# High and low weight halves laid element by element beside each other in the feature-major blocks of a hybrid decoder layer

## The chip, the cores and the metric

The kernel runs on one core of one Trainium2 chip. The time is device microseconds of that core, the median over several runs. A profile of one execution on the chip gives, for every instruction, its engine, start and duration; the engines are named PE (TensorE, matmuls), PEld (TensorE's weight loads), DVE (VectorE), ACT (ScalarE), POOL (GpSimd) and SP (the queue that issues the loads from memory).

## The reference

One decoder layer over 256 tokens of 2,048 features, in float32: a mixer that runs an mLSTM and an RWKV-7 branch in parallel and merges them with sigmoid gates, a cross-attention into 256 memory tokens, and a channel mixer (a convolution of width 3 over tokens, a gated GELU). Each part is normed before and after and added to the residual stream.

```python
def reference(x, mem, ...):
    h = rms_norm(x, mix_pre_norm[l])
    y = hybrid_mixer(h, w_in[l], ...)              # 2048 -> 10536 columns, two recurrences, w_branch_a/b, w_out
    x = x + rms_norm(y, mix_post_norm[l])
    h = rms_norm(x, xattn_pre_norm[l])
    m = rms_norm(mem, mem_norm[l])
    x = x + rms_norm(cross_attention(h, m, xattn_wq[l], xattn_wkv[l], xattn_wo[l]), xattn_post_norm[l])
    h = rms_norm(x, ffn_pre_norm[l])
    x = x + rms_norm(conv_glu_ffn(h, ffn_w_up[l], ffn_conv_w[l], ffn_conv_b[l], ffn_w_down[l]), ffn_post_norm[l])
    return x

def conv_glu_ffn(h, w_up, conv_w, conv_b, w_down):
    u = h @ w_up                                   # 2048 -> 16384
    uc = conv_b + sum(conv_w[j] * shift_right(u, CONV_WIDTH - 1 - j) for j in range(CONV_WIDTH))
    gate, up = split_cols(uc, (D_FF, D_FF))
    return (jax.nn.gelu(gate, approximate=True) * up) @ w_down
```

Almost all of the arithmetic is products of 256 tokens with large weight matrices, which are read once from memory.

## The kernel before

**Split products.** TensorE multiplies in a reduced float32 format (`float32r`). To keep accuracy, every operand is split into a high half (rounded to that format) and a low half (the rest), and a product is three matmuls: high weight with high activation, high weight with low activation, low weight with high activation. All three add up in PSUM.

**Blocks and chunks.** The weights come in chunks of 512 KB, 128 partitions x 1,024 float32. `run()` goes through a list of blocks, and each block through its chunks. A block is of one of two kinds. In a feature-major block (`fm`) the weights are the stationary operand: TensorE loads 128 x 128 weights and streams 256 tokens (`hh`, `hl`, `fh`, `fl`, ...) past them, so the output has features on partitions. A chunk holds two rows of contraction (`kj`) by 512 features, so 2 x 4 x 3 = 24 matmuls of 256 columns. In a token-major block (`tm`) the activations are stationary and the weights stream, 512 columns at a time. Most of the kernel is feature-major: the mixer's input projection in large part, gates, branch and output projections, and the FFN's up projection; the FFN's down projection is token-major and ends the program.

**The path of a chunk.** `Feed.dma` issues its load into a `raw` buffer (four of them). `Feed.hi` has ScalarE cast it to the high half, `wh`; `Feed.lo` has VectorE subtract the cast from `raw` into the low half, `wl`. `run()` calls `feed.lo(i + 3)` while it works on chunk `i`, so the halves are made two to three chunks ahead. `wh` and `wl` are separate pools of four buffers, each of 1,152 float32 per partition; a cast waits until the matmuls have read the `wh` four chunks back, a subtraction until they have read the `wl` four chunks back, and the subtraction also waits for its own cast. The order of all instructions is written out by the program (there is no scheduler): `Spread` deals the side work of evacuations and the recurrences out between matmuls by a fixed budget of costs.

**Where a half lies in its buffer.** `Feed.staged` (L374) puts the 1,024 values of a half not at the buffer's start but `o` elements behind it: 0 in token-major blocks with 512 or more columns, 16 elsewhere (64 bytes). The buffers and the activations that the matmuls stream all start at a multiple of 128 bytes. For 19 chunks of the program a table `KICK` (L342), indexed by the chunk's number, shifts it otherwise: kind 0 puts the first row at 24 elements and the second 24 further than usual, kind 1 puts only the second row 8 further, kind 2 puts both at 24. All entries lie below chunk 244, so before the long run of the FFN's up projection is under way.

Of the kernel before, what the change touches and what calls it, by code (L numbers as in the profile page):

```python
# [10 lines left out]
F32R = mybir.dt.float32r  # L11
# [4 lines left out]
P = 128  # L16
# [129 lines left out]
def _layer(ctx, tc, nc, d, dbg):  # L146
# [5 lines left out]
    wp = ctx.enter_context(tc.tile_pool(name="wp", bufs=4))  # L152
# [9 lines left out]
    def big(name, shape=None, dt=F32):  # L162
        return mp.tile(shape or [P, KD, S], dt, tag="big", bufs=2, name=name)
# [79 lines left out]
    class Stat:  # L243


        def __init__(self, name, tag="ysb1", sq="au", apart=False):
            self.name, self.tag, self.sq, self.apart = name, tag, sq, apart
            self.rc = cp.tile([P, 2], F32, name=name + "_c")
            self.n = 0
            self.done = False  # L250
# [94 lines left out]
    class Feed:  # L345
        def __init__(self, order):
            self.kind = [k for k, s in order]
            self.src = [s for k, s in order]
            self.raw, self.st, self.nd, self.ns, self.nl = {}, {}, 0, 0, 0

            self.sm = [big(f"w0{i}", [P, 4, 2, 512]) for i in range(2)]

# [21 lines left out]
        def staged(self, name, r, i):  # L374


            k, c = r.shape[1:]
            kick = KICK.get(i)
            e = -(-c // 64) * 64
            o = 0 if c >= 512 and self.kind[i] == "tm" else 16  # L380
            if kick is not None:
                o, e = ((24, e + 24), (o, e + 8), (24, e))[kick]
            w = wp.tile([P, 1024 + 128], F32R, tag=name, bufs=4, name=name)
            return w[:, o:o + k * e].rearrange("p (k c) -> p k c", k=k)[:, :, 0:c]

        def hi(self, upto):
# [1714 lines left out]
```

## Time and profile before

| | |
|---|---|
| time, median of 3 runs (lowest, highest) | 1866.33 us (1866.29, 1867.76) |
| span of the profiled execution, first to last instruction | 1863.2 us |
| granted TensorE clock in it | 0.999 |
| matmuls | 14,934, TensorE busy 1853.5 us |
| VectorE busy | 1295.5 us, of which the 639 subtractions into `wl` (L421) 774.8 us |
| ScalarE busy | 1017.0 us, of which the 639 casts into `wh` (L391) 663.6 us |
| loads from memory | 347.01 MB, 187 GB/s over the span |

The profiled execution is one run of its own; its span is from the first to the last instruction and leaves out what lies around them. In the rows of the profile, the names stand as output<-inputs with the moving operand before the stationary one, so `fm<-fh,wh` is a feature-major matmul that streams `fh` past weights `wh`. Matmuls overlap in the pipeline: a duration of 277 ns for one says how long it was in flight, and the pace is what starts are apart. Nearly all matmuls stand under the one line of the helper that issues them (L181), so they are told apart by their tiles.

### The profile page before, as it was taken

Reading aid. Unit: us, or ns where it says so; the run is one execution under the profiler, and the core shown is the slowest. Engines: PE = TensorE matmul, PEld = TensorE weight load, DVE = VectorE, ACT = ScalarE, POOL = GpSimd, SP = SyncE. Lnnn points to the kernel's source line nnn. Section 1 sums busy time; section 2 is a strip of 40 time slices with the busy share of each in tenths; the row PEclk is TensorE's granted clock in tenths of the full one; section 3 lists DMA queues with packets and bytes.
Section 4 is the critical chain, followed back from the end, with each engine's and each line's share of the span. In section 5 each row is a group of like instructions: output and inputs, shape, how many; then the busy total and the mean of one; then the engine's idle time right before and its main releaser. Section 6 shows DMA issues by size and latency. Waiting matters only on the chain.

```text
span 1863.2 us, 36212 instructions
## 1 busy us (share of the span) xinstructions
PE 1853.5 (99%) x14934; PEld 1767.5 (95%) x14934; DVE 1295.5 (70%) x1832; ACT 1017.0 (55%) x1492; POOL 32.4 (2%) x62
## 2 busy tenths in 40 slices
PE   9999999999999999999999999999999999999998
PEld 9999988999999999999999999999999988888887
DVE  7789777566675857787766667776666775556555
ACT  6876445655454646665554455444445554545544
POOL 0000020000000000000000000000000000000000
PEclk9999999999999999999999999999999999999999
DMA  7556544344555765555666666666666666666664
GB/s 261 186 166 203 180 149 160 136 160 158 172 195 196 277 197 180 165 180 172 202 192 194 196 195 196 185 194 199 195 194 195 197 192 215 194 193 192 194 192 145
DMA packets 98198, 351.47 MB, mean 189 GB/s; under 512 B 11056, under 2 KB 11568, under 8 KB 97648
## 3 DMA queue, kind: packets, MB, share of 16 engines
q1 hardware_dynamic: 97168, 348.01, 58.6%
q8 instruction: 117, 1.92, 0.4%
q10 hardware_dynamic: 864, 1.15, 0.2%
q14 instruction: 49, 0.40, 0.1%
HBM read 347.01 MB, written 2.10 MB: 187 GB/s over the span
## 4 chain that ended last, share of the span: by engine, by line
PE 98%; DVE 1%; DMA 0%; issue 0%; ACT 0%; ACTq 0%; DVEq 0%
PE fm L181 68%; PE tm L181 25%; PE gram L181 0%; DVE wl L421 0%; PE Y L181 0%; DMA w<-in_w_in_dram 0%; PE num L181 0%; PE lv L181 0%; DVE ql L66 0%; PE X L181 0%; PE U L181 0%; PE zg L181 0%; DVE z L66 0%; PE zwa L181 0%; PE xsc L181 0%
## 5 line engine op out<-in xcount | busy, mean ns | idle before, releaser
L421 DVE TENSOR_TENSOR wl<-raw,wh 128x1024 fp32r<-128x1024 f32 (+1 forms) x639 | 774.8, 1218 | 412.7 <-ACT wh L391 406.5
L391 ACT CAST wh<-raw 128x1024 fp32r<-128x1024 f32 (+1 forms) x639 | 663.6, 1043 | 476.0 <-PE fm L181 362.5
L181 PE MATMUL fm<-fh,wh 128*128 128x256 f32 x2048 | 564.2, 277 | 0.6 <-DVE fh L66 0.6
L181 PE MATMUL fm<-fh,wl 128*128 128x256 f32 x2048 | 563.2, 276 | 0.0
L181 PE MATMUL fm<-fl,wh 128*128 128x256 f32 x2048 | 563.2, 276 | 0.0
L181 PEld LDWEIGHTS fm<-fh,wh 128*128 128x128 f32 x2048 | 383.6, 188 | 0.8 <-DVE fh L66 0.8
L181 PEld LDWEIGHTS fm<-fl,wh 128*128 128x128 f32 x2048 | 383.5, 188 | 0.0
L181 PEld LDWEIGHTS fm<-fh,wl 128*128 128x128 f32 x2048 | 383.5, 188 | 0.0
L181 PE MATMUL tm<-wh,as 128*128 128x512 f32 x1024 | 315.1, 389 | 0.0
L181 PE MATMUL fm<-hh,wh 128*128 128x256 f32 x1024 | 284.3, 280 | 1.7 <-ACT wh L402 1.5
L181 PE MATMUL fm<-hl,wh 128*128 128x256 f32 x1024 | 281.7, 277 | 0.0
L181 PE MATMUL fm<-hh,wl 128*128 128x256 f32 x1024 | 281.5, 277 | 0.1
L181 PEld LDWEIGHTS tm<-wh,as 128*128 128x128 f32 x1024 | 192.2, 188 | 39.8
L181 PE MATMUL tm<-wl,as 128*128 128x512 f32 x512 | 199.2, 389 | 0.0
L181 PEld LDWEIGHTS fm<-hh,wh 128*128 128x128 f32 x1024 | 191.9, 188 | 3.4 <-ACT wh L402 1.7
L181 PEld LDWEIGHTS fm<-hl,wh 128*128 128x128 f32 x1024 | 191.9, 188 | 0.1
L181 PEld LDWEIGHTS fm<-hh,wl 128*128 128x128 f32 x1024 | 191.5, 188 | 0.3 <-DVE wl L421 0.3
L181 PEld LDWEIGHTS tm<-wl,as 128*128 128x128 f32 x512 | 96.1, 188 | 19.9
L66 ACT CAST as<-ac 128x256 fp32r<-128x256 f32 x128 | 45.6, 404 | 110.8 <-PE tm L181 110.8
L66 DVE TENSOR_TENSOR as<-ac,as 128x256 fp32r<-128x256 f32 x128 | 48.6, 421 | 61.7 <-ACT as L66 61.7
L181 PE MATMUL fm<-mgh,wh 128*128 128x256 f32 x256 | 70.9, 277 | 0.0
L181 PE MATMUL fm<-mgl,wh 128*128 128x256 f32 x256 | 70.8, 276 | 0.0
(406 smaller groups left out, 2225.0 us busy)
## 6 DMA issues: line engine op xcount, KB each, us to landing
raw<-in_w_fu_dram SPq DMA_DIRECT2D x256, 512.0 KB, 4.1
raw<-in_w_in_dram SPq DMA_DIRECT2D x152, 512.0 KB, 3.6
raw<-in_w_fd_dram SPq DMA_DIRECT2D x128, 512.0 KB, 3.9
raw<-in_w_br_dram SPq DMA_DIRECT2D x32, 512.0 KB, 4.1
raw<-in_w_mo_dram SPq DMA_DIRECT2D x32, 512.0 KB, 4.3
raw<-in_w_xk_dram SPq DMA_DIRECT2D x8, 512.0 KB, 4.2
raw<-in_w_xv_dram SPq DMA_DIRECT2D x8, 512.0 KB, 3.6
raw<-in_w_xq_dram SPq DMA_DIRECT2D x8, 512.0 KB, 4.0
```

The costliest lines, as they stand in the source:

```text
L66: return f(out, *a, **k)
L181: pe.matmul(out, lhsT, rhs, start=start, stop=stop, skip_group_check=True)
L391: nc.scalar.copy(wh, r)
L421: nc.vector.tensor_sub(wl, r, self.st[self.nl][0])
```

## The change

The two halves of a chunk get one buffer of 2,304 float32 instead of two of 1,152, from a pool of four (`w2`), allocated when the high half is made. In a feature-major chunk the high value and the low value of one weight are neighbours: high at even places, low at odd ones. Each half is then a view with a step of two elements, and so a weight load of 128 columns reads every second float32, 8 bytes apart, over 1,024 bytes. The cast writes, and the subtraction reads and writes, with the same step. The chunk starts 16 elements (64 bytes) into its buffer as before, or 24 if the table `KICK` has an entry for it, of whichever kind; the second row no longer has a shift of its own. In the other chunks the two halves lie one behind the other in the shared buffer and keep their offsets and kinds of shift. Sizes, the number of instructions and their order on every engine stay as they are.

```diff
@@ class Feed
             self.raw, self.st, self.nd, self.ns, self.nl = {}, {}, 0, 0, 0
+            self.pairs = {}
...
@@ def staged(self, name, r, i):
             k, c = r.shape[1:]
             kick = KICK.get(i)
             e = -(-c // 64) * 64
+            if name == "wh":
+                self.pairs[i] = wp.tile([P, 2304], F32R, tag="w2", bufs=4, name="w2")
+            w = self.pairs[i]
+            if self.kind[i] == "fm":
+                o = 16 if kick is None else 24
+                return w[:, o:o + 2 * k * e].rearrange("p (k c i) -> p k c i", k=k, i=2)[:, :, 0:c, name == "wl"]
             o = 0 if c >= 512 and self.kind[i] == "tm" else 16
             if kick is not None:
                 o, e = ((24, e + 24), (o, e + 8), (24, e))[kick]
-            w = wp.tile([P, 1024 + 128], F32R, tag=name, bufs=4, name=name)
+            w = w[:, 0:1152] if name == "wh" else w[:, 1152:2304]
             return w[:, o:o + k * e].rearrange("p (k c) -> p k c", k=k)[:, :, 0:c]
```

What waits for what shifts a little with the shared buffer. On VectorE, in the FFN's up projection, two subtractions with the work between them stood like this before (`raw` is the loaded chunk, `us` and `fm` belong to the evacuation of a finished block, and the names in brackets are what the instruction waits for):

```order
L421 TENSOR_TENSOR wl<-raw,wh 128x1024 [waits DMAHW4_49,PE_49,Activation_49]
L66 TENSOR_TENSOR us<-fm,stf_b 128x512 [waits PE_49]
L421 TENSOR_TENSOR wl<-raw,wh 128x1024 [waits DMAHW5_49,PE_49,Activation_49]
L66 TENSOR_TENSOR us<-fm,stf_b 128x512
L66 SCALAR_TENSOR_TENSOR tg<-us,cv,tg 128x255 [waits Activation_49]
```

and stand like this now:

```order
L428 TENSOR_TENSOR w_17711<-raw,w_17711 128x1024 [waits DMAHW4_49,Activation_49]
L66 TENSOR_TENSOR us<-fm,stf_b 128x512 [waits PE_49]
L428 TENSOR_TENSOR w_17749<-raw,w_17749 128x1024 [waits DMAHW5_49,Activation_49]
L66 TENSOR_TENSOR us<-fm,stf_b 128x512
L66 SCALAR_TENSOR_TENSOR tg<-us,cv,tg 128x255 [waits Activation_49]
```

The order is unchanged; the subtraction no longer waits for TensorE itself, since its buffer was already free when the cast before it wrote there. The cast in turn waits for one matmul more than before, the last that reads the low half of the chunk four back.

## The prediction

> **What bounds the kernel now.** I read the head of the page first, then its chain that ended last.
>
> ```profile
> span 1863.2 us, 36212 instructions
> PE 1853.5 (99%) x14934; PEld 1767.5 (95%) x14934; DVE 1295.5 (70%) x1832; ACT 1017.0 (55%) x1492; POOL 32.4 (2%) x62
> PEclk9999999999999999999999999999999999999999
> PE 98%; DVE 1%; DMA 0%; issue 0%; ACT 0%; ACTq 0%; DVEq 0%
> ```
>
> TensorE is busy 99% of the span at a full granted clock, and 98% of the chain is TensorE. Next is what TensorE itself waited for: the view of waits, TensorE's rows.
>
> ```profile
> PE fm L181 <- ACT wh L402: 1.5, 1, 1.5
> PE warm L181 <- POOL ones L210: 1.1, 1, 1.1
> PE fm L181 <- ACT wh L391: 0.2, 1, 0.2
> ```
>
> The three columns are microseconds in total, times, and the longest. After the first chunk, TensorE never waits for a weight half in any amount that counts. So only the pace of the matmuls can move the time. The chain in order of time gives that pace:
>
> ```profile
> 529.91 127.96 PE fm L181 x1128
> ...
> 938.94 568.50 PE fm L181 x5016
> 1507.44 348.20 PE tm L181 x1536
> ```
>
> One unbroken stretch of feature-major matmuls (names `fm`, 256 moving columns) takes 568.50/5016 = 113.3 ns each; the token-major one (`tm`, 512 columns) takes 348.20/1536 = 226.7 ns. The second is twice the first although each has one weight load of 128 columns. A pace proportional to the moving columns, 0.443 ns per column in both, is the pace of the moving stream; a pace set by weight loads would be the same in both. That is the main reading on which the forecast rests.
>
> How much room is left for the weight load, next? Weight loads by form (mean ns behind the busy time):
>
> ```profile
> L181 PEld LDWEIGHTS fm<-fh,wh 128*128 128x128 f32 x2048 | 383.6, 188 | 0.8 <-DVE fh L66 0.8
> L181 PEld LDWEIGHTS gbc<-g,id 4*128 4x128 f32 x8 | 1.0, 182 | 0.1
> L181 PEld LDWEIGHTS Y<-T,KR 64*64 64x64 f32 x96 | 3.0, 134 | 0.2
> L181 PEld LDWEIGHTS lv<-mt,m 32*32 32x32 f32 x128 | 2.3, 107 | 0.3
> ```
>
> From 32 to 64 columns a load grows by 27 ns, from 64 to 128 by 54 ns: 0.84 ns per column, and about 80 ns that overlap with the load before. 128 columns stream in 54/64 x 128 = 108 ns, against 113.3 ns of moving. The cover is thin: 5 ns, or 5% of a load's stream. A load that became 6% slower would set the pace.
>
> And the weight load can disturb the moving stream even when it is short enough. TensorE in order of time, the first and the last of 37 consecutive matmuls, and then of 16:
>
> ```profile
> 431.02 0.28 PE L181 MATMUL fm<-hh,wl 128*128 128x256 f32 x1
> ...
> 435.25 0.28 PE L181 MATMUL fm<-hh,wl 128*128 128x256 f32 x1
> ```
>
> ```profile
> 50.56 0.28 PE L181 MATMUL fm<-hh,wh 128*128 128x256 f32 x1
> ...
> 52.37 0.28 PE L181 MATMUL fm<-hh,wh 128*128 128x256 f32 x1
> ```
>
> 4.23 us over 36 gaps is 117.5 ns; 1.81 us over 15 gaps is 120.7 ns. The second stretch, and the later half of the first, are chunks 18 and 138, whose weights the table `KICK` (L342) puts 96 bytes behind a 128-byte boundary in place of 64. The code gives those matmuls no other difference, so the two reads of TensorE do interact, by where the weights lie against the moving operand. The earlier half of the first stretch (chunk 137, unshifted) is slow too: it follows 32 small matmuls. It looks as if TensorE could fall out of step after an interruption and stay so until a shifted chunk.
>
> **The change, part by part.** First its reach: every matmul that writes an `fm` tile.
>
> ```profile
> 0.00:1864.00 1864.00, 1301.41 (x11328) 1.00 0.59 189
> 938.90:1507.40 568.50, 568.50 (x5016) 1.00 0.63 194
> 0.00:938.90 938.90, 732.87 (x6313) 1.00 0.56 185
> ```
>
> These rows are busy time by stretch of the matmuls on `fm`: 11,328 in all. Each of their weight loads now reads 128 values over 1,024 bytes instead of 512. One nanosecond more per load, once the cover of 5 ns is gone, is 11.3 us.
>
> *The 8-byte step itself.* No matmul in this trace has weights with a step of two elements. The nearest row on one side is `gbc`, whose weights have step zero (one element, read 128 times): 182 ns against 188 for 128 neighbouring ones, so the load's time does not depend on how many bytes 128 columns cover, at least downwards. On the other side the nearest rows are the two out-of-step stretches: +4.2 ns (117.5 - 113.3) and +7.4 ns (120.7 - 113.3) per matmul, which on 11,328 matmuls is +48 and +84 us. I take the value of the first, no extra time, since a load that takes one value per step of 0.84 ns is what the 32-, 64- and 128-column rows and the step-zero row all show; both ends stay in the range.
> The Trainium skill, "SBUF — State Buffer", Specifications (TRN2), speaks against the change: SBUF lines are 16 bytes, at least two hits per line are needed for full bandwidth, and each new line costs. At 8 bytes a line still gets exactly two float32 hits, so by the letter the sum stays at zero, while the new lines per load double; no run here shows the line size.
> The same page, Who interferes with whom, calls the matmul and weight-load ports independent and says TensorE waits on nobody. The two stretches above disagree, with 117.5 and 120.7 ns against 113.3; by the rule alone the change would be worth exactly zero.
>
> *Pace of the two reads.* The moving operand steps 4 bytes per 0.443 ns, 9.0 bytes per ns. The weights stepped 4 bytes per 0.84 ns, half as fast; now they step 8, 9.5 bytes per ns, nearly equal. A fixed offset (64 bytes as before; 68 for the low half) then holds through the whole load. Either the two never meet, and the slow stretches go, or they meet all the time. What the first is worth: the table has 19 entries of 24 matmuls or less, 19 x 24 x 4.2 ns = 1.9 us, and some unshifted stretches beside them; an upper bound is everything that feature-major matmuls lose before 938.9 us, 732.87 - 6313 x 0.1133 = 17.6 us, most of it refills behind small matmuls that the change does not touch. I put it at 3 us, near the lower end, because a stretch of 1,128 matmuls there (127.96 us, 113.4 ns each) already runs at full pace.
>
> *The shifts.* In feature-major chunks three kinds of shift become one (24 elements, 96 bytes). Cost as now: 0.1 us each if they slow their own chunk.
>
> *Writes and waits.* The cast and the subtraction write every second element, and the subtraction reads so. Rows of the steady stretch, in order of time:
>
> ```profile
> 1195.65 1.23 DVE L421 TENSOR_TENSOR wl<-raw,wh 128x1024 fp32r<-128x1024 f32 x1 [1.50 <-ACT wh L391]
> 1197.28 1.05 ACT L391 CAST wh<-raw 128x1024 fp32r<-128x1024 f32 x1 [1.67 <-PE fm L181]
> 1000.00:1400.00 400.00, 400.00 (x3532) 400.00 (x3531) 274.62 (x365) 199.69 (x256) 0.00 (x0) 1.00 0.64 194
> ```
>
> A chunk is 24 x 113.3 ns = 2.72 us of TensorE, and 400 us hold 147 chunks. VectorE is busy 274.62 of the 400, ScalarE 199.69, so a subtraction could grow by (400 - 274.62)/147 = 0.85 us and a cast by 1.36 us before they set the pace. Below nothing there is no gain: neither is waited for. I take zero. If the subtraction doubled, VectorE would need 274.62 + 147 x 1.23 = 455 us for 400: 14% on 568 us, about +78 us.
> Waits: high and low half now share one buffer, so a cast waits for the last low-half matmul of the chunk four back, one matmul (0.11 us; 0.23 in token-major) later than now; the subtraction no longer waits for TensorE, being behind the cast already. Behind the cast on ScalarE stand the next casts; they are needed some two chunks (5 us) later, so 0.23 us is hidden. The order of instructions is the same on every engine.
>
> *Sum.* 11,328 x 0 - (0 to 3 us) + 0. The profiled span is 1863.2 us, 3.1 us under the 1866.33 median, which lies outside the first and last instruction; so 1862 of span, about 1865 us.
>
> **The rivals.**
> - *Out of step for long (slower).* Nothing ties the single 96-byte shift to the places where TensorE falls out of step with the new pace. For: chunk 137 shows that an unshifted chunk can be slow from start to end. Against: most unshifted chunks are not. Place: the long stretch from 938.94; price 5016 x 4.2 ns = 21 us, so 1887; it decides if the last interruption before that stretch leaves TensorE out of step.
> - *The weight load becomes the bound (slower).* From 6% more time per load, in all feature-major matmuls. For: the cover is 5 ns and the load covers twice the bytes; the moving stream, which already covers that many bytes, needs 113.3 ns for them. Against: the step-zero row. Price by the first stretch +48 us, 1914; by the second +84 us, 1950; one value per two of today's steps would be +0.84 x 128 = +108 ns, less 5 of cover, 1.2 ms, which I give next to nothing.
> - *The floor falls (faster).* If the 113.3 ns were itself the price of two reads colliding, matmuls could go down to the load's 108 ns: 11,328 x 5.3 = 60 us, 1806. Against: the 512-column matmuls pay the same per column with half as many loads.
> - *All losses before 938.9 us vanish (faster):* at most 17.6 us, 1849.
> - *VectorE's strided subtraction doubles (slower):* +78 us, 1944.
>
> **How the numbers follow.** About 0.2%, 3.7 us, is what a measurement of this kernel can tell from no change. Forecast, 1862.6 to 1870: 0.44. Out of step for long: 0.20. Load-bound: 0.18, of which 0.11 up to 1920. Floor falls: 0.10. All losses vanish: 0.05. VectorE: 0.03. So faster 0.10 + 0.05 = 0.15, within 0.2% 0.44, slower 0.20 + 0.18 + 0.03 = 0.41. The range 1850 to 1920 holds the forecast, the first rival, the cheaper part of the second and nearly all of the lost-time case: 0.44 + 0.20 + 0.11 + 0.05 = 0.80. The forecast's own range is 1862 to 1867.
>
> **What would show it.** Right: the long feature-major piece of the chain stays at 568 us for 5,016 matmuls, weight loads stay at 188 ns, and VectorE's subtraction at 1.23 us. Slow stretches gone: chunks 137 and 18 at 113 ns. Out of step: the same long piece at 117 ns or more in part. Load-bound: every `fm` matmul above 113.3 ns from the first chunk on, with longer weight loads and token-major matmuls unchanged at 226.7. Floor fallen: the piece under 560 us. What would make me wrong outright is a pace of the feature-major matmuls other than 113.3 ns in the long stretch.

## The result, and the profile after

The changed kernel takes 1936.14 us (median of 4 runs, 1935.76 to 1936.47); the kernel before took 1866.31 us beside it (median of 4). The ratio is 1.0375, 95% interval 1.036 to 1.039: 70 us slower, where about no change was forecast, and above the range of 1850 to 1920.

The head of the page and its chain, of the kernel after:

```profile
span 1934.0 us, 36171 instructions
PE 1925.6 (100%) x14934; PEld 1839.6 (95%) x14934; DVE 1297.5 (67%) x1832; ACT 1064.0 (55%) x1492; POOL 32.2 (2%) x62
PEclk9999999999999999999999999999999999999999
PE 99%; DMA 0%; ACT 0%; DVE 0%; ACTq 0%; issue 0%; DVEq 0%
```

TensorE is still the whole chain at the full granted clock, so the 70.8 us by which the span grew are matmuls that start further apart. The chain in order of time says which:

```profile
547.02 135.38 PE fm L181 x1128
...
976.09 601.92 PE fm L181 x5016
1578.01 348.44 PE tm L181 x1536
```

The long feature-major piece went from 568.50 to 601.92 us: 601.92/5016 = 120.0 ns a matmul in place of 113.3. The shorter one has the same pace, 135.38/1128 = 120.0. The token-major piece, whose loads the change leaves alone, stands at 348.44/1536 = 226.8 ns as before. The busy time of all matmuls on `fm`, and the forms of their weight loads:

```profile
0.00:1934.00 1934.00, 1373.75 (x11328) 1.00 0.58 182
```

```profile
L181 PEld LDWEIGHTS fm<-fh,w 128*128 128x128 f32 x4096 | 646.1, 194 | 0.8 <-DVE fh L66 0.8
L181 PEld LDWEIGHTS tm<-w,as 128*128 128x128 f32 x1536 | 288.1, 188 | 60.1 <-DVE w L428 0.3
```

The feature-major matmuls were busy 1301.41 us and are busy 1373.75: 72.3 us more, which is the whole loss. That is 6.4 ns for each of 11,328; the pace changed by 6.7 where it had been at its best. Their weight loads take 194 ns in place of 188, while those of the token-major matmuls stay at 188. The two other engines, by the groups of the page after, and last the cast of the page before:

```profile
L428 DVE TENSOR_TENSOR w<-raw,w 128x1024 fp32r<-128x1024 f32 (+1 forms) x639 | 775.7, 1218 | 492.2 <-ACT w L398 490.6
L398 ACT CAST w<-raw 128x1024 fp32r<-128x1024 f32 (+1 forms) x639 | 707.8, 1113 | 524.6 <-PE fm L181 394.4
L391 ACT CAST wh<-raw 128x1024 fp32r<-128x1024 f32 (+1 forms) x639 | 663.6, 1043 | 476.0 <-PE fm L181 362.5
```

The subtraction costs 1218 ns, as it did before, with a step in what it reads and writes. The cast grew from 1043 to 1113 ns, but ScalarE idles more than before, waiting for TensorE. Neither is what TensorE waits for.

### The profile page after: what moved, and what is told of

It is laid out like the page before. It is cut to its first block, busy times and chain, and to the rows that moved or that the text cites. A ratio compares the mean times of both kernels' runs of the same rounds, so it can differ in the third digit from the quotient of the medians.

```text
span 1934.0 us, 36171 instructions
## 1 busy us (share of the span) xinstructions
PE 1925.6 (100%) x14934; PEld 1839.6 (95%) x14934; DVE 1297.5 (67%) x1832; ACT 1064.0 (55%) x1492; POOL 32.2 (2%) x62
## 4 chain that ended last, share of the span: by engine, by line
PE 99%; DMA 0%; ACT 0%; DVE 0%; ACTq 0%; issue 0%; DVEq 0%
PE fm L181 70%; PE tm L181 24%; PE gram L181 0%; PE Y L181 0%; DMA w<-in_w_in_dram 0%; PE num L181 0%; PE lv L181 0%; PE X L181 0%; PE U L181 0%; PE zg L181 0%; PE xsc L181 0%; PE zwa L181 0%; PE xt L1927 0%; PE Tn L181 0%; PE stb L181 0%; PE xo L181 0%
## 5 line engine op out<-in xcount | busy, mean ns | idle before, releaser
L428 DVE TENSOR_TENSOR w<-raw,w 128x1024 fp32r<-128x1024 f32 (+1 forms) x639 | 775.7, 1218 | 492.2 <-ACT w L398 490.6
L398 ACT CAST w<-raw 128x1024 fp32r<-128x1024 f32 (+1 forms) x639 | 707.8, 1113 | 524.6 <-PE fm L181 394.4
L181 PE MATMUL fm<-fh,w 128*128 128x256 f32 x4096 | 738.5, 282 | 0.6 <-DVE fh L66 0.6
L181 PEld LDWEIGHTS fm<-fh,w 128*128 128x128 f32 x4096 | 646.1, 194 | 0.8 <-DVE fh L66 0.8
L181 PE MATMUL fm<-fl,w 128*128 128x256 f32 x2048 | 576.4, 282 | 0.0
L181 PEld LDWEIGHTS fm<-fl,w 128*128 128x128 f32 x2048 | 396.3, 194 | 0.0
L181 PE MATMUL fm<-hh,w 128*128 128x256 f32 x2048 | 376.6, 284 | 0.5 <-ACT w L409 0.3
L181 PE MATMUL tm<-w,as 128*128 128x512 f32 x1536 | 348.6, 389 | 0.0
L181 PEld LDWEIGHTS tm<-w,as 128*128 128x128 f32 x1536 | 288.1, 188 | 60.1 <-DVE w L428 0.3
L181 PEld LDWEIGHTS fm<-hh,w 128*128 128x128 f32 x2048 | 324.2, 195 | 2.4 <-ACT w L409 0.5
```

The costliest lines, as they stand in the source:

```text
L181: pe.matmul(out, lhsT, rhs, start=start, stop=stop, skip_group_check=True)
L398: nc.scalar.copy(wh, r)
L428: nc.vector.tensor_sub(wl, r, self.st[self.nl][0])
```

## The experiments

After the result there were two theories. **Load**: a load with 8-byte steps is longer by itself than the 113.3 ns in which 256 columns move, and so sets the pace. **Collision**: the load reads more places, and each costs the moving stream something, however long that stream is.

**1. Only the shared buffer.** In the changed kernel, the interleave is taken out; both halves lie in one buffer, one behind the other.

```diff
-            if self.kind[i] == "fm":
-                o = 16 if kick is None else 24
-                return w[:, o:o + 2 * k * e].rearrange("p (k c i) -> p k c i", k=k, i=2)[:, :, 0:c, name == "wl"]
```

> The changed kernel without the interleave: one shared buffer per chunk, high half in front, low half behind it, with the offsets and all three kinds of shift of the kernel before. If the 8-byte step is the whole cause, this takes the time before, 1866 us within 2, and the long feature-major piece is back at 568 us for 5,016 matmuls. If the shared buffer (later casts) or the lost kinds of shift carry part of the 70 us, the time lies between 1870 and 1936.

Measured: 1866.83 us, ratio to the kernel before 1.0004 (0.9994 to 1.0013). The long piece in the chain:

```profile
940.82 568.50 PE fm L181 x5016
```

The later casts of the shared buffer cost nothing. So all of the 70 us belong to the interleave, with what it does to the places of the weights.

**2. The step where 512 columns move.** In the kernel before, the stationary activations of the FFN's down projection are interleaved instead.

```diff
-            a = a.rearrange("p (i j s) -> p i j s", i=2, j=2)
+            a = a.rearrange("p (j s i) -> p i j s", i=2, j=2)
```

> The kernel before, with the step put somewhere else: in the FFN's down projection, where the stationary operand is the activation and 512 columns move, the two halves of the activations lie element by element, so that those 1,536 loads step 8 bytes. Theory 'load': a load at 8 bytes needs 120 ns, too long for 256 moving columns (113.3) but not for 512 (226.7); these matmuls stay at 226.7 ns and the time at 1866 within 2. Theory 'collision': each load at 8 bytes takes 6.7 ns from the moving stream however long that is; these matmuls go to 233.4 ns, the piece of 1,536 from 348 to 358 us, and the time to about 1876.

Measured: 1875.76 us, ratio 1.0053 (1.0036 to 1.007). The chain in order of time:

```profile
939.53 568.50 PE fm L181 x5016
1508.03 358.42 PE tm L181 x1536
```

358.42/1536 = 233.3 ns: each load adds 6.7 ns to a matmul that has 227 ns to hide it. So the load theory alone cannot be right; something of the collision kind is there.

**3. The step alone, block by block.** In the kernel before, the host lays the columns of the FFN's up weights in another order, and the load picks them up with a step. Buffers, casts and subtractions are as before.

```diff
+    STEP = [1, 1] + [(1, 2, 4, 8, 1, 2)[i // 5] for i in range(30)]
+
+    def cols_of(w, kj, m, s):
+        if s == 1:
+            return w[:, kj, m * P:(m + 1) * P]
+        if s < 8:
+            g = m // s * s * P + m % s
+            return w[:, kj, g:g + (P - 1) * s + 1:s]
+        return w.rearrange("p k c -> p (k c)")[:, kj * 4 + m:kj * 4 + m + (P - 1) * 8 + 1:8]
...
-                            a, c = wh[:, kj, m * P:(m + 1) * P], wl[:, kj, m * P:(m + 1) * P]
+                            a, c = (cols_of(w, kj, m, b.get("step", 1)) for w in (wh, wl))
...
+        fu["step"] = STEP[b]
...
+    for n in range(30):
+        s, v = (1, 2, 4, 8, 1, 2)[n // 5], o["w_fu"][n + 2]
+        if s in (2, 4):
+            o["w_fu"][n + 2] = v.reshape(v.shape[0], P, 2, 4 // s, s, P).swapaxes(-1, -2).reshape(v.shape)
+        elif s == 8:
+            o["w_fu"][n + 2] = v.reshape(v.shape[0], P, 8, P).swapaxes(-1, -2).reshape(v.shape)
```

> The kernel before with separate buffers and unit-step writes; only the columns of the FFN's up weights lie permuted, so that the loads of its blocks 2 to 31 step 4, 8, 16, 32, 4 and 8 bytes, five blocks (960 matmuls) each. Both theories: blocks at 4 bytes 113.3 ns, blocks at 8 bytes 120.0 (then writes with a step and the shared buffer have no part in it). Load 'by 64-byte piece' (0.83 ns for each of 8, 16, 32, 64 pieces on top of 106.7): 133 ns at 16 bytes and 160 at 32. Load 'by 16-byte line' (0.21 ns for each of 32, 64, 128, 128 lines): 133 ns at both 16 and 32. Collision, one TensorE cycle of 0.417 ns for each 64-byte piece on top of 106.7 plus 6.7: 127 and 140. Time by the first about 1866 + 13 + 19 + 45 = 1943, by the second 1917, by the third 1905.

Measured: 2116.55 us (one run). Pieces of the chain inside the blocks with 8, 16, 32, 4 and again 8 bytes, in this order:

```profile
962.97 90.12 PE fm L181 x751
1079.81 220.24 PE fm L181 x935
1306.00 224.21 PE fm L181 x931
1539.92 100.19 PE fm L181 x884
1644.93 110.16 PE fm L181 x918
```

That is 120.0, 235.6, 240.8, 113.3 and 120.0 ns. The 8-byte step gives 120.0 ns without any write with a step, so the casts have no part in it. At 16 bytes the pace doubles, which neither theory had: the three counts in the expectation had put 16 bytes at 127 to 133 ns, and the program at 1905 to 1943. The Trainium skill, "SBUF — State Buffer", Specifications (TRN2), says that a 16-byte line needs two hits for full bandwidth: 235.6 ns at one float32 per line against 120.0 at two agrees with where it sets the edge; that two hits give full bandwidth does not agree, at 120.0 against 113.3.

**4. Half the moving columns.** The same kernel, with each of those matmuls cut in two of 128 columns.

```diff
-                                mm(*w)
+                                if "step" in b and b not in entry:
+                                    mm(w[0][:, 0:P], w[1], w[2][:, 0:P], w[3], w[4])
+                                    mm(w[0][:, P:S], w[1], w[2][:, P:S], False, w[4])
+                                else:
+                                    mm(*w)
```

> The last kernel with each feature-major matmul of the FFN's up blocks 2 to 31 cut into two of 128 moving columns, each with its own load, so that the load alone sets the pace (128 columns move in 57 ns). Load theory: 113 ns or less a matmul at 4 bytes, 120 at 8, 133 at 16, 160 or 133 at 32, whatever moves. Collision theory: the moving stream is there only half of the time, so the loads run at their bare 107 to 109 ns with less than half of the extra: 107 to 110 at 4 bytes, 109 to 113 at 8. 11,520 matmuls in place of 5,760: in all about 2600 to 2700 us.

Measured: 3385.05 us (one run), far over what was expected, for a reason that the windows by stretch show (the time of the stretch, the busy time and count of PE's weight loads, then the granted clock, DMA share and GB/s):

```profile
1030.00:1290.00 260.00, 260.00 (x2192) 1.00 0.29 92
1400.00:1640.00 240.00, 240.00 (x1030) 0.50 0.15 49
2210.00:2600.00 390.00, 390.00 (x1830) 0.50 0.16 52
```

From the first block at 16 bytes on, the granted clock was half, to the end of the cut blocks. The first two steps ran at full clock, in these pieces of the chain (4 bytes, 8 bytes):

```profile
1027.94 38.08 PE fm L181 x341
1069.94 220.08 PE fm L181 x1834
```

38.08/341 = 111.7 ns and 220.08/1834 = 120.0 ns. So with 128 columns to move a load at 4 bytes takes 111.7 and one at 8 bytes 120.0: here the load theory holds and the collision theory, which expected 109 to 113, falls. Both effects exist, then, and the next runs take them apart.

At half the clock the pieces inside the blocks with 16, 32, 4 and 8 bytes are these:

```profile
1399.98 240.10 PE fm L181 x1029
1747.91 452.16 PE fm L181 x1884
2209.84 390.19 PE fm L181 x1829
2619.87 380.16 PE fm L181 x1782
```

That is 233.3, 240.0, 213.3 and 213.3 ns. The loads at 16 and 32 bytes take no longer than at full clock in the third experiment (235.6 and 240.8), while those at 4 and 8 bytes become equal.

**5 and 8. Sixteen places.** The place of the chunk in its buffer changes along the FFN's up projection, once in the changed kernel (step 8), once in the kernel before (step 4). The edit in the kernel before is this; in the changed kernel the same places are set inside its feature-major branch.

```diff
+            if i >= 264 and self.kind[i] == "fm":
+                o = (16, 0, 2, 4, 8, 12, 16, 18, 20, 24, 28, 32, 40, 48, 56, 16)[(i - 264) // 16]
```

> The changed kernel; in the FFN's up projection the place of the chunk in its buffer goes through 16 values, 16 chunks (384 matmuls) each: 64, 0, 8, 16, 32, 48, 64, 72, 80, 96, 112, 128, 160, 192, 224, 64 bytes. If the 120.0 ns are the load's own time, no place is faster than 120, and places off a 64-byte boundary are the same or slower by a piece (0.8 ns). If they are collisions with the moving operand, some place gets 113.3 ns, and others more than 120.

> The kernel before (step 4 bytes, separate buffers); the place of each half in its buffer goes through the same 16 values as in the fifth experiment: 64, 0, 8, 16, 32, 48, 64, 72, 80, 96, 112, 128, 160, 192, 224, 64 bytes. If the load at 4 bytes is short enough by itself and only collisions cost, places that are multiples of 64 bytes get 113.3 ns and others 117 to 121; if place doesn't matter by itself and the shifted chunks were slow only by having been shifted, all get 113.3 after their first chunk. Time between 1866 and about 1890.

Measured: 1938.14 us for step 8 and 1889.52 us for step 4, one run each. Pieces of the chain at step 8, in groups at 16, 48, 64, 80, 96 and 112 bytes:

```profile
981.00 40.11 PE fm L181 x338
1072.90 40.21 PE fm L181 x331
1119.89 40.20 PE fm L181 x335
1211.92 40.10 PE fm L181 x338
1257.98 40.08 PE fm L181 x334
1303.96 42.10 PE fm L181 x346
```

and at step 4, at 0, 32, 64, 192 and again 64 bytes:

```profile
883.60 11.52 PE fm L181 x96
...
991.95 40.12 PE fm L181 x339
1081.97 40.12 PE fm L181 x354
1399.92 40.16 PE fm L181 x341
1489.98 40.12 PE fm L181 x354
```

At step 8: 118.7, 121.5, 120.0, 118.6, 120.0 and 121.7 ns; no place of all those tried comes under 118. At step 4: 120.0, 118.3, 113.3, 117.8 and 113.3; the places not shown lie between 115.7 ns (8 bytes) and 120.0. Place matters at both steps. At step 4, of the places tried, 64 bytes alone gets the 113.3 ns on which the kernel before runs, and gets them at once when the kernel comes there from a slow place; 0 and 192 bytes do not, so it isn't simply a multiple of 64. Neither side of the two expectations held in full: at step 8 two places are faster than 120 but none gets 113.3, and at step 4 place matters by itself but not by multiples of 64.

**6. Places under 512 moving columns.** The same for the stationary activations of the FFN's down projection, with both steps.

```diff
+    AS = ((1, 0), (1, 8), (1, 16), (1, 24), (2, 0), (2, 2), (2, 4), (2, 8), (2, 12), (2, 16), (2, 20), (2, 24), (2, 28), (2, 32), (2, 48), (1, 4))
...
-                a = mp.tile([P, 1024 + 128], F32R, tag=f"au{n % 2}", bufs=1, name="as")[:, 0:1024]
-            a = a.rearrange("p (i j s) -> p i j s", i=2, j=2)
+                s, o = AS[k // 8]
+                a = mp.tile([P, 1024 + 128], F32R, tag=f"au{n % 2}", bufs=1, name="as")[:, o:o + 1024]
+            if AS[k // 8][0] == 2:
+                a = a.rearrange("p (j s i) -> p i j s", i=2, j=2)
+            else:
+                a = a.rearrange("p (i j s) -> p i j s", i=2, j=2)
```

> The kernel before; in the FFN's down projection (512 moving columns, so a load of 120 ns can't be the bound) the stationary activations go through 16 layouts, 8 rows of contraction (96 matmuls) each: step 4 bytes at 0, 32, 64, 96 bytes, then step 8 bytes at 0, 8, 16, 32, 48, 64, 80, 96, 112, 128, 192 bytes, then step 4 at 16 bytes. If what the second experiment showed (233.4 ns in place of 226.7) are collisions that depend on how the two reads lie, some places of step 8 get 226.7 and some of step 4 get 230 or more; if each 64-byte piece that a load enters costs the moving stream one cycle of 0.417 ns at any place, all of step 8 are at 233.4 and all of step 4 at 226.7 to 230, alike.

Measured: 1872.17 us (one run). Pieces of the chain: step 4 at 0 and at 64 bytes, step 8 at 0 and at 64 bytes.

```profile
1506.85 20.19 PE tm L181 x89
1550.81 20.30 PE tm L181 x87
1596.86 20.30 PE tm L181 x87
1707.90 20.24 PE tm L181 x88
```

226.9, 233.3, 233.3 and 230.0 ns. So the 6.7 ns of the second experiment are nothing peculiar to the 8-byte step: a 4-byte load in the wrong place costs about as much (233.3 at 64 bytes against 226.9 at 0). A load of 120 ns would be hidden behind 512 columns, so this is not the load's own length but a collision, and it depends on place. At step 8 no place is back at 226.7: over all eleven the starts stand 230.0 to 233.3 ns apart.

**7. Few moving columns.** Single blocks cut into pieces of 64, 32 and 16 columns, each with its own load.

```diff
+    PLAN = {4: (1, 64), 6: (2, 64), 8: (1, 32), 10: (2, 32), 12: (1, 16), 14: (2, 16), 20: (4, 64), 24: (8, 64)}
...
-                                mm(*w)
+                                for c in range(0, S, n):
+                                    mm(w[0][:, c:c + n], w[1], w[2][:, c:c + n], w[3] and c == 0, w[4])
...
```

> The kernel before; single blocks of the FFN's up projection with the matmuls cut into pieces of 64, 32 or 16 moving columns, each with its own load, at a step of 4 or 8 bytes, and two with 64 columns at 16 and 32 bytes; whole blocks of 256 columns at 4 bytes between them. If a load at 8 bytes needs 120.0 ns by itself, it does at 64, 32 and 16 columns too, and a load at 4 bytes some 107 to 112 ns. If the extra comes from meeting the moving operand, both fall towards 107 as fewer columns move, and towards each other. Loads at 16 and 32 bytes: 233 and 240 ns, as with 256 columns, if they are the load's own.

Measured: 4341.86 us (one run), again because the clock fell soon after the start of each cut block. What counts are the first microseconds of such blocks, at the full clock. Windows (time, TensorE busy, count, granted clock, DMA share, GB/s): step 4 and step 8 with 64 columns at their start.

```profile
895.50:898.50 3.00, 3.00 (x30) 1.00 0.93 350
1081.50:1084.50 3.00, 3.00 (x28) 1.00 0.52 175
```

and, again of the first such block, the stretch that begins 4.5 us after its start:

```profile
900.00:940.00 40.00, 40.00 (x194) 0.51 0.11 38
```

Pieces of the chain at the start of the blocks with 64 columns (4 and 8 bytes), with 32 columns (4 and 8) and with 16 columns (4 and 8):

```profile
895.84 3.13 PE fm L181 x28
1081.82 2.59 PE fm L181 x22
...
1265.96 3.13 PE fm L181 x28
1613.77 3.65 PE fm L181 x31
...
1962.40 3.13 PE fm L181 x28
2638.76 2.71 PE fm L181 x23
```

At 4 bytes that is 111.8 ns with 64, with 32 and with 16 columns; at 8 bytes 117.7, 117.7 and 117.8 (64 columns move in 28 ns at the pace of the long stretch, 64 x 0.443). Neither falls as fewer columns move, so the load itself takes 6 ns more with the longer step. The 120.0 ns of the fourth experiment, at the same place with 128 columns, hold 2.3 ns more, which are put down to collisions. The two blocks with 64 columns at 16 and 32 bytes start like this, at full clock:

```profile
3401.49 4.43 PE fm L181 x19
3647.80 3.82 PE fm L181 x16
```

233.2 and 238.8 ns, as was expected of the load's own time.

**9 and 10. The two causes in whole programs.** The changed kernel with its chunks at 80 bytes, and the kernel before with its chunks at byte 0.

```diff
-                o = 16 if kick is None else 24
+                o = 20
```

```diff
-            o = 0 if c >= 512 and self.kind[i] == "tm" else 16
+            o = 0 if c >= 512 and self.kind[i] in ("tm", "fm") else 16
```

> The changed kernel with every feature-major chunk 80 bytes into its buffer in place of 64 (no shifted ones). In the sweep over places this was the best for a step of 8 bytes, 118.7 ns against 120.0. If the load's own time (117.7 ns at 8 bytes with few moving columns) is the floor and place only adds to it, the whole program gains 11,328 x 1.3 ns = 15 us on the changed kernel: about 1921, and still 55 above the kernel before. If the place matters only block by block, the time stays near 1936.

> The kernel before (step 4 bytes) with feature-major chunks at byte 0 of their buffers in place of 64. In the sweep this place cost 121.2 ns in place of 113.3. If place alone makes the kernel before fast, all feature-major matmuls lose about 7 ns: 11,328 x 7.4 = 84 us, about 1950, more than the change cost. If the load at 4 bytes is short enough wherever it lies, the time stays at 1866.

Measured: 1916.94 us for the first, ratio to the kernel before 1.0278 (1.0261 to 1.0296); 1934.64 us for the second, ratio 1.0374 (1.0358 to 1.0389). The long piece of the chain, of the first and of the second:

```profile
969.12 590.78 PE fm L181 x5016
```

```profile
975.60 601.91 PE fm L181 x5016
```

The other long feature-major piece of the first, and the weight loads of the second:

```profile
543.38 133.86 PE fm L181 x1128
```

```profile
L181 PEld LDWEIGHTS fm<-fh,wh 128*128 128x128 f32 x2048 | 392.2, 192 | 0.8 <-DVE fh L66 0.8
```

The first runs at 590.78/5016 = 117.8 ns. That is the load's own 117.7, so in this piece nothing of the collisions is left, and no place tried went below it. It beats its expectation of 118.7 ns a matmul (and of 1921 us). But place in the buffer does not decide alone: at the same 80 bytes the other long piece runs at 133.86/1128 = 118.7 ns, and the group in the sweep at 118.6. What else decides is open.

The second runs at 120.0 ns with loads of 4-byte steps. The kernel before, put at another place, is as slow as the changed one. The expectation of 1950 us had taken 121.2 ns for this place, where the chain has 120.0. The loads take 192 ns here in place of 188, so a longer duration of a weight load is no sure mark of a longer step.

What the loads collide with was only argued so far, since moving the weights also moves what ScalarE and VectorE write. The trace of the second run settles part of it: between 1000 and 1570 us, 4,748 of 4,749 gaps between starts of matmuls are 120 ns, and one is 119. ScalarE, VectorE and the transfers from memory come and go in that time (in its first 400 us ScalarE is busy 193 us and VectorE 263), so they are not what costs the time. The stream of the moving operand, which is always there, is left; no run moved it. A load that is longer by itself at byte 0 was not tried with few columns to move; the sixth experiment, where 227 ns would hide it, speaks against that.

No version tried is faster than the kernel before.

## Why the prediction was wrong

**What bounds the kernel** was read rightly: TensorE's pace was all, 113.3 ns was the moving stream, and token-major matmuls stayed at 226.8 ns.

**The step that failed is the first term of the sum**, the 8-byte step at "no extra time", taken from the step-zero row. A load at 8 bytes takes 6 ns more (111.8 to 117.7 ns, the seventh experiment), which is more than the moving stream covers. Step zero reads one place over and over; it was the nearest row but on the wrong side, since it could not show what more places cost. That row also reads 4 partitions in place of 128, and its 182 ns were taken as equal to 188, although 6 ns are the size of what the change cost per load.

**The cover was mis-sized too.** From the durations of loads of 32, 64 and 128 columns the prediction had 108 ns of stream and 5 ns of cover. With few columns to move, loads stand 111.7 to 111.8 ns apart, so the cover was 113.3 - 111.7 = 1.6 ns. A slope over the number of columns leaves out what each load costs beside its columns. The prediction had said that a load 6% longer would set the pace; the load became 5% longer, and did.

**The sum as the runs give it.** Load above moving stream: 117.7 - 113.3 = 4.4 ns, on 11,328 matmuls 50 us. Collisions at the place of 64 bytes: 120.0 - 117.7 = 2.3 ns, or 26 us. Together they are 76 us, against the 72.3 us that the feature-major matmuls lost; matmuls that had run slower than 113.3 ns in the kernel before had less to lose. Of whole programs, the ninth experiment, with few collisions left, measures 1916.94 - 1864.9 = 52 us for the load, and the changed kernel lies 1936.14 - 1916.94 = 19 us above it.

**The rivals.** "The weight load becomes the bound" is what happened, with its mark: every `fm` matmul slower from the first chunk on, longer loads, token-major ones unchanged. It was priced at 1914 to 1950 by the two out-of-step stretches, and the result lies between them, near the middle. That is in part luck: those stretches are slow by place, at a 4-byte step, and not because a load is too long. The mark of longer loads does not tell the two apart either, as the tenth run's 192 ns show. The rival was given 0.18, and the range left out its dearer part, 0.07 of that. "Out of step for long" did not happen: the pace is even, and not slow in stretches. "The floor falls" and "all losses vanish" were wrong in direction. VectorE's subtraction did not change, 1218 ns.

**Pace of the two reads.** That a fixed offset through the whole load would mean they never meet, or always, was not borne out as put: at step 8 the places tried range from 118.6 to 121.7 ns, with 117.8 in the ninth run. The stretches at chunks 18 and 138 that had been read as "out of step" are of the kind that place makes: at step 4, the places other than 64 bytes give 115.7 to 120.0 ns, against 117.5 and 120.7 there. That chunk 137, which lies at 64 bytes, was slow in the kernel before is not explained by place, like the two paces at 80 bytes in the ninth run; no run took that apart.

**Writes and waits**, put at nothing, were right. The cast grew by 70 ns, inside the 1.36 us of room, and the shared buffer alone measured 1.0004.

## What to carry to other kernels

Where a weight load hides behind the moving operand, size its cover by letting the load set the pace (few moving columns, at the full clock), not by the slope of its durations: here that shows 1.6 ns of room where the slope had 5. A row for an access with no step says nothing of a wider one; if the trace has no nearer row, the forecast should lean to the costlier end where the cover is thin and the count is in the thousands. And where two operands are read at once, their places in memory are part of the tuning: moving the weights by 64 bytes cost as much here as the whole change.

## What the runs showed of the hardware that was not expected

- A weight load of 128 float32 takes 111.8 ns at 4-byte steps, 117.7 at 8, and then doubles: 233.2 ns at 16 and 238.8 at 32 bytes (pace of matmuls with 64 columns at full clock; with 256 columns the last two are 235.6 and 240.8).
- The place of the weights against the moving operand is worth some 6 to 7 ns a matmul, both for 256 columns (113.3 to 120.0) and for 512 (226.9 to 233.3), and at 4-byte steps a good place for one is a bad one for the other: 64 bytes gives 113.3 and 233.3, 0 bytes 120.0 and 226.9. What in the addresses decides is open: 64 and 192 bytes differ (113.3 and 117.8), and 80 bytes at step 8 ran at 117.8 and at 118.7 in one program.
- The granted clock fell to 0.50 some 5 us into a block of matmuls with 64 columns, and in the blocks of 128 columns at 16 bytes, though TensorE was busy all the time by the profile. It stayed full with 128 columns at 4 and 8 bytes, and with 256 columns at 16 bytes. By the pace of 0.443 ns per column, the moving stream filled about half of the time where the clock stayed full (57 of 112 to 120 ns, 113 of 236) and a quarter where it fell (28 of 112, 57 of 233); that this share is what counts was not tested.
- At half clock a load takes 213.3 ns with 4-byte and with 8-byte steps alike, while loads at 16 and 32 bytes take 233.3 and 240.0 ns, about what they take at full clock (the fourth experiment).
- ScalarE's cast to a step of 8 bytes took 1113 ns in place of 1043; VectorE's subtraction, with a step in one input and the output, the same 1218.
